# A mixture-of-experts stage on one Trainium2 core: later pairs of experts fetch their tokens by indirect loads and transpositions, from places that a table in DRAM lists

## The chip, the cores and the metric

The kernel runs on one core of one Trainium2 chip. The metric is the device time of one execution in microseconds (us), as the median of several runs. The engines are called PE (TensorE; PEld is its weight load), DVE (VectorE), ACT (ScalarE), POOL (GpSimd) and SP (SyncE, which here only issues the weight loads). Line numbers such as L1071 are those of the kernel before unless the text says that they are of the change.

## What is computed

The program takes 512 tokens of width 1024 in fp32 through two blocks of layers. The first block has a layer of attention with a SwiGLU feed-forward part and a layer of a short convolution with a mixture of experts; the second block has four mixers of other kinds. The change lies in the mixture of experts, cut here to what matters:

```python
D_MODEL, SEQ, N_EXPERTS, TOP_K, D_FF_EXPERT = 1024, 512, 8, 2, 1408

def moe_swiglu(x, w_router, b_router, w_gate, w_up, w_down):
    xt = x.reshape(T, D)
    logits = (xt @ w_router) + b_router
    top_logit, top_e = lax.top_k(logits, TOP_K)
    top_w = jax.nn.softmax(top_logit, axis=-1)
    ...
    def one_block(args):
        e, toks, w = args
        xb = xt[toks]
        h = jax.nn.silu(xb @ w_gate[e]) * (xb @ w_up[e])
        return (h @ w_down[e]) * w[:, None]
    ...
    y = jnp.zeros((T, D)).at[tok_buf].add(out)
```

Each token goes to its two best experts of eight; the two results are weighted and added to the residual stream.

## The kernel before

**Precision.** An fp32 product is made of three matmuls of a faster type: each operand is split into `hi` (rounded, on ACT, L97 and L99) and `lo` (the rest, on DVE, L109 and L113, or on POOL, L111).

**Places.** Each expert has 160 places (`CAP`), of which 128 are the main block and 32 are called the others. If an expert has more tokens than that, `beyond` computes the rest under a branch; here the branch is passed without it. The branch (`most`) is taken by every engine.

**Entry.** `moe` ranks the logits on DVE (L986 to L997: `gt`, `tie`, `rank`, `on`), counts places by matmuls with a triangle (L1002 to L1005, `pos`, `most`), computes the two softmax weights `wts`, and writes four numbers for each token and expert into `know`. Meanwhile the residual stream is transposed to token order (L1022) and split into eight pairs `xth`, `xtl`.

**Dispatch.** `dispatch(e)` serves the experts e and e+1. DVE makes one-hot tiles from `posm` (L1169); 64 matmuls with them (L1178, L1179) pick the tokens out of `xth` and `xtl`; `places` turns each of the 16 results into a hi (ACT), a lo (DVE) and a copy of the others' columns (ACT, L1065). Small matmuls of `know` with the one-hots (L1188, L1191) give the token numbers and weights of each place, and some 16 short DVE operations make `rows` (where results are scattered) and `wt` of them. Pair 0 is dispatched ahead of expert 0; the pairs 2, 4 and 6 within expert 1, 3 and 5, between its up and its down stage.

**Experts.** `up` takes 24 weight loads (16 of 512 KB, 8 of 384 KB), `down` takes 11 of 512 KB. Each load goes from SP's queue into a `raw` tile, is split, and feeds six matmuls for the main block (L1071 to L1073); four matmuls for the others (L1081) use the raw tile itself, and stand collected in groups of four loads. A raw tile is free for the next load when its L1081 matmuls are done. Every third lo of `up` is on POOL (`MO_UP = "pvv"`), every lo of `down` on DVE. Results are scattered by indirect POOL DMAs into `ys` in DRAM (L1232, L1238).

**End.** Ahead of expert 7, POOL loads the sums so far from `ys` (16 loads, L1219) and adds them in pairs (8 additions, L1220); in the middle of the last down stage `mid` transposes them and adds them to the residual stream. Expert 7's own result does not go through `ys`: one-hots `OH` (L1252, L1257) put it in place by matmuls.

The order of the instructions on each engine is set by a tile scheduler, which may move an instruction ahead of others within its window; pools of buffers (`A`: 28 tiles, `T`: 8, PSUM: 8 banks) set the waits.

Of the kernel before, what the change touches and what calls it, by code (L numbers as in the profile page):

```python
# [20 lines left out]
S = 512  # L21
# [914 lines left out]
def moe_begin(s):  # L936
# [15 lines left out]
    m["spot"] = s.ldm("c_spot", (128, 3))  # L952
    m["tok"] = s.ldm("c_tok", (128, NT))
# [17 lines left out]
def moe(s):  # L971
# [25 lines left out]
    nc.vector.tensor_scalar(on, rank, 2.0, None, ALU.is_lt)  # L997
# [18 lines left out]

    xt = []
    for i in range(NT):
        for hf in range(2):
            ps = s.P(("sc", "tp")[hf])  # L1020
            for k in range(4):
                nc.tensor.transpose(ps[:, k * 128:k * 128 + 128], s.xT[4 * hf + k][:, i * 128:i * 128 + 128], s.ident)  # L1022
            h = s.xp.tile([128, 512], F32R, name="xth", tag="xh")
            l = s.xp.tile([128, 512], F32R, name="xtl", tag="xl")
            s.split(ps, h, l, scale=s.rt[:, i:i + 1])
            xt.append((h, l))
# [19 lines left out]
    know = mixp.tile([128, NT, NE, 4], F32R, name="know")  # L1046
    nc.vector.scalar_tensor_tensor(know[:, :, :, 0], sel[1], float(S), m["tok"].unsqueeze(2).to_broadcast(rank3), ALU.mult, ALU.add)
    nc.vector.memset(know[:, :, :, 1].bitcast(F32), 1.0)
    u, v = s.small(rank3, tag="selu"), s.small(rank3, tag="selv")
    nc.vector.tensor_mul(u, sel[0], wts[:, 0].unsqueeze(2).to_broadcast(rank3))  # L1050
    nc.vector.tensor_mul(v, sel[1], wts[:, 1].unsqueeze(2).to_broadcast(rank3))
    nc.vector.tensor_add(u, u, v)
    nc.vector.tensor_copy(know[:, :, :, 2], u)
    nc.vector.tensor_sub(know[:, :, :, 3], u, know[:, :, :, 2].bitcast(F32))

    def places(X, ps, k):
# [7 lines left out]
        s.split(ps[:, 0:128], t[:, 0], t[:, 1], scale=g)  # L1064
        nc.scalar.activation(X[0][:, n * k:n * k + n], ps[:, 128:CAP], AF.Copy, scale=g)  # L1065
# [18 lines left out]
    def up(gu, X, first=()):  # L1084
# [3 lines left out]
        for c, (f0, nb) in enumerate(FBLK):  # L1088
            n = nb * 128
            pp, po, held = [s.P("mm"), s.P("sc")], s.P("o"), []  # L1090
            for k in range(KT):
                i = KT * c + k
                wh, wl, raw = first.pop(0) if first else load3(gu(i)[:, :2 * n], MO_UP[i % len(MO_UP)])
# [27 lines left out]
    def down(dn, H, put, puto, mid=None):  # L1121
# [3 lines left out]
        for f in range(FE):  # L1125
# [9 lines left out]
            if f == FE // 2 and mid is not None:  # L1135
                mid()
# [18 lines left out]

    most = nc.values_load(mosti[0:1, 0:1], min_val=0, max_val=S)
# [4 lines left out]
    def dispatch(e):  # L1161
        YR = float(YROWS)
        tok = s.small((128, 2), tag="etok", bufs=1)

        oh = []
        for i in range(NT):
            t = s.T((128, 2, CAP), F32R)
# [3 lines left out]
        X = [[], []]  # L1171
        for k in range(KT):
            ps = s.P(("st", "o", "tp", "sc", "tp", "sc", "st", "o")[k] if e == 0 else ("st", "o")[k % 2])
            for i in range(NT):
                h, l = xt[2 * i + k // 4]
                q = slice((k % 4) * 128, (k % 4) * 128 + 128)
                r = oh[i].rearrange("p a b -> p (a b)")
                nc.tensor.matmul(ps[:, :2 * CAP], h[:, q], r, start=i == 0, stop=False)  # L1178
                nc.tensor.matmul(ps[:, :2 * CAP], l[:, q], r, start=False, stop=i == NT - 1)  # L1179
            for x in range(2):  # L1180
                places(X[x], ps[:, x * CAP:x * CAP + CAP], k)
        info = []
        for x in range(2):
            ps = s.P("st")
            rows = s.small((128, 3), I32, tag="erow", bufs=4)
            wt = s.small((128, 2), tag="ewt", bufs=4)
            for i in range(NT):
                nc.tensor.matmul(ps[:, 0:4], oh[i][:, x, 0:128], know[:, i, e + x], start=i == 0, stop=i == NT - 1)  # L1188
            for i in range(NT):
                for j in range(4):  # L1190
                    nc.tensor.matmul(ps[32 * j:32 * j + 32, 4:8], oh[i][:, x, 128:].bitcast(F32), know[:, i, e + x].bitcast(F32),  # L1191
                                     start=i == 0, stop=i == NT - 1)
            for b in range(2):
                k4 = s.small((128, 4), tag="ek4")
                t = s.small((128, 1), tag="et")
                nc.vector.tensor_copy(k4, ps[:, 4 * b:4 * b + 4])

                nc.vector.scalar_tensor_tensor(t, k4[:, 1:2], m["spot"][:, b:b + 1], k4[:, 0:1], ALU.mult, ALU.subtract)
                nc.vector.tensor_scalar(t, t, m["spot"][:, b:b + 1], -1.0, ALU.subtract, ALU.mult)
                if b == 0:  # L1200
                    nc.vector.tensor_copy(rows[:, 0:1], t)
                    nc.vector.tensor_scalar(rows[:, 1:2], t, YR, None, ALU.add)
                else:
                    nc.vector.tensor_scalar(rows[:, 2:3], t, 2.0, m["spot"][:, 2:3], ALU.mult, ALU.add)
                nc.vector.tensor_add(wt[:, b:b + 1], k4[:, 2:3], k4[:, 3:4])
                if e + x == NE - 1:

                    f = s.small((128, 1), tag="etf")
                    nc.vector.tensor_scalar(f, t, float(S), -float(S), ALU.is_ge, ALU.mult)
                    nc.vector.tensor_add(tok[:, b:b + 1], t, f)  # L1210
            info.append((rows, wt))
        return X, info, tok


    def load(hf, i):
# [4 lines left out]
        nc.gpsimd.tensor_add(y[0], y[0], y[1])  # L1220
        return y[0]

    for e in range(NE):
        if e == 0:
            X, info, tok = dispatch(0)
        H = up(lambda i, e=e: a["moe_gu"][e * KT * len(FBLK) + i], X[e % 2], ahead)
        rows, wt = info[e % 2]

        def put(x, ps, rows=rows, wt=wt):
            yt = s.T()  # L1230
            nc.scalar.activation(yt, ps, AF.Copy, scale=wt[:, 0:1])
            nc.gpsimd.indirect_dma_start(out=s.ys[:, :], out_offset=bass.IndirectOffsetOnAxis(ap=rows[:, x:x + 1], axis=0),  # L1232
                                         in_=yt[:, :], in_offset=None)

        def puto(ps, rows=rows, wt=wt):
# [5 lines left out]
        if e % 2 and e + 1 < NE:  # L1241
            X, info, tok = dispatch(e + 1)
# [1018 lines left out]
```

## Time and profile before

| | us |
|---|---|
| median of 3 runs | 2858.03 |
| the runs | 2858.03, 2867.24, 2856.01 |
| profiled execution, its own time | 2853.54 |
| its span | 2851.8 |
| experts 0 to 7 in it, from the first L1071 matmul to the last one | 988.5 to 1604.8 |

The profile is of one execution, which is 4.5 us shorter than the median. Its page gives totals over the whole span; the mixture of experts is about a fifth of it and is read from the trace by stretches: an expert begins with its first L1071 matmul. "Idle before" in a row of a group or a timeline is the time in which that engine did nothing ahead of the instruction, and the arrow names what ended it.

### The profile page before, as it was taken

What the parts mean: (1) busy time and instruction counts of PE and PEld (TensorE: products, weight loads), DVE (VectorE), ACT (ScalarE), POOL (GpSimd) and SP (SyncE); (2) the same over time, 40 slices, a digit from 0 to 9 for tenths busy, and PEclk for the clock granted to TensorE, in tenths of its full rate; (3) what the DMA queues carried; (4) which work ended last, traced back from release to release, by engine and by line L of the source; (5) the groups of instructions that cost most, each with busy time, mean ns of one, the idle gap of its engine ahead of it and who ended that gap; (6) DMA issues with size and microseconds to landing.
All of it is one profiled execution on the core that took longest, in us unless ns stands there. A gap on an engine that the chain in (4) does not pass through costs nothing.

```text
span 2851.8 us, 40111 instructions
## 1 busy us (share of the span) xinstructions
PE 2735.7 (96%) x15211; PEld 2168.5 (76%) x15211; DVE 1719.8 (60%) x3194; ACT 1223.3 (43%) x2017; POOL 695.0 (24%) x526
## 2 busy tenths in 40 slices
PE   7989999999999899999998999999999998999999
PEld 6766678888888667676765786778888886788887
DVE  3667669465555465656655747677375456775573
ACT  3555653223322455655654424444243234443342
POOL 3310024222312122323334321032023130122120
PEclk9979999999999899999999999999999998999999
DMA  3210123334432075757757633132333420232322
GB/s 131 93 30 20 37 74 125 102 114 158 174 98 82 24 253 183 279 207 252 254 215 295 188 113 79 32 110 85 107 96 101 131 72 15 83 96 84 108 91 94
DMA packets 119788, 348.36 MB, mean 122 GB/s; under 512 B 16322, under 2 KB 27874, under 8 KB 119076
## 3 DMA queue, kind: packets, MB, share of 16 engines
q1 hardware_dynamic: 106352, 316.66, 33.6%
q0 software_dynamic: 7904, 24.93, 2.5%
q10 hardware_dynamic: 5332, 4.14, 0.5%
q8 instruction: 121, 1.98, 0.3%
q14 instruction: 79, 0.65, 0.1%
HBM read 326.66 MB, written 19.01 MB: 121 GB/s over the span
## 4 chain that ended last, share of the span: by engine, by line
PE 58%; DVE 3%; DMA 2%; ACT 1%; issue 1%; POOL 1%; ACTq 0%; POOLq 0%; SPq 0%; DVEq 0%
PE psmm L138 5%; PE psmm L139 5%; PE psmm L140 5%; PE pso L1081 4%; PE pstp L140 3%; PE pstp L139 3%; PE pstp L138 3%; PE pssc L140 3%; PE pssc L139 3%; PE pssc L138 3%; PE psmm L1071 2%; PE psmm L1072 2%; PE psmm L1073 2%; PE pssc L1073 2%; PE pssc L1072 2%; PE pssc L1071 2%
## 5 line engine op out<-in xcount | busy, mean ns | idle before, releaser
L97 ACT ACTIVATE whi<-raw 128x1024 fp32r<-128x1024 f32 (+5 forms) x663 | 625.7, 947 | 1001.4 <-PE psmm L139 331.6
L113 DVE TENSOR_TENSOR wlo<-raw,whi 128x1024 fp32r<-128x1024 f32 (+4 forms) x581 | 723.3, 1251 | 426.4 <-ACT whi L97 420.0
L111 POOL TENSOR_TENSOR wlo<-raw,whi 128x1024 fp32r<-128x1024 f32 (+3 forms) x82 | 181.4, 2213 | 490.8 <-ACT whi L97 467.7
L138 PE MATMUL psmm<-xh,whi 128*128 128x512 f32 x688 | 273.6, 399 | 10.1 <-ACT xh L99 8.3
L139 PE MATMUL psmm<-xl,whi 128*128 128x512 f32 x688 | 271.8, 395 | 2.3 <-DVE xl L109 2.3
L140 PE MATMUL psmm<-xh,wlo 128*128 128x512 f32 x688 | 271.7, 395 | 1.0 <-DVE wlo L113 1.0
L139 PE MATMUL pssc<-xl,whi 128*128 128x512 f32 x448 | 174.9, 390 | 0.0
L140 PE MATMUL pssc<-xh,wlo 128*128 128x512 f32 x448 | 174.8, 390 | 0.0
L138 PE MATMUL pssc<-xh,whi 128*128 128x512 f32 x448 | 174.6, 390 | 0.0
L138 PEld LDWEIGHTS psmm<-xh,whi 128*128 128x128 f32 x688 | 130.5, 190 | 39.6 <-ACT xh L99 8.3
L1971 POOL TENSOR_TENSOR T<-T 128x512 f32<-128x512 f32 x44 | 57.0, 1296 | 415.8 <-DVE T L1968 352.9
L139 PE MATMUL pstp<-xl,whi 128*128 128x512 f32 x400 | 155.9, 390 | 0.0
L138 PE MATMUL pstp<-xh,whi 128*128 128x512 f32 x400 | 155.7, 389 | 0.0
L140 PE MATMUL pstp<-xh,wlo 128*128 128x512 f32 x400 | 155.7, 389 | 0.0
L139 PEld LDWEIGHTS psmm<-xl,whi 128*128 128x128 f32 x688 | 130.4, 190 | 31.6 <-DVE xl L109 4.9
L1081 PE MATMUL pso<-raw,A 128*32 128x256 f32 x2112 | 153.4, 386 | 0.8 <-ACT A L1065 0.8
L140 PEld LDWEIGHTS psmm<-xh,wlo 128*128 128x128 f32 x688 | 130.4, 189 | 28.9 <-DVE wlo L113 1.5
L111 POOL TENSOR_TENSOR A<-T,A 128x512 fp32r<-128x512 f32 (+1 forms) x78 | 125.6, 1610 | 100.7 <-ACT A L97 100.5
L1071 PE MATMUL psmm<-whi,A 128*128 128x512 f32 (+1 forms) x280 | 114.3, 408 | 9.1 <-ACT whi L97 9.1
L1072 PE MATMUL psmm<-wlo,A 128*128 128x512 f32 (+1 forms) x280 | 113.1, 404 | 10.0 <-DVE wlo L113 8.0
L1081 PEld LDWEIGHTS pso<-raw,A 128*32 128x32 f32 x2112 | 68.1, 110 | 68.4 <-issue 28.5
L254 DVE TENSOR_TENSOR xT<-psmm,xT 128x512 f32<-128x512 f32 x90 | 61.8, 687 | 90.1 <-PE psmm L140 89.6
(651 smaller groups left out, 6151.5 us busy)
## 6 DMA issues: line engine op xcount, KB each, us to landing
raw<-moe_gu SPq DMA_DIRECT2D x128, 512.0 KB
raw<-moe_dn SPq DMA_DIRECT2D x88, 512.0 KB
raw<-w_up_t SPq DMA_DIRECT2D x88, 512.0 KB
raw<-moe_gu SPq DMA_DIRECT2D x64, 384.0 KB
raw<-ffn_gu SPq DMA_DIRECT2D x44, 512.0 KB
raw<-od_w_in_t SPq DMA_DIRECT2D x24, 512.0 KB
raw<-w_in_t SPq DMA_DIRECT2D x24, 512.0 KB
raw<-w_down_t SPq DMA_DIRECT2D x32, 384.0 KB
```

The lines of the kernel that those rows point to most:

```text
L97: nc.scalar.activation(out, x, AF.Copy)
L111: nc.gpsimd.tensor_sub(out, x, h.bitcast(F32))
L113: nc.vector.tensor_sub(out, x, h.bitcast(F32))
L138: nc.tensor.matmul(ps, wh, xh, start=first, stop=False)
L139: nc.tensor.matmul(ps, wh, xl, start=False, stop=False)
L140: nc.tensor.matmul(ps, wl, xh, start=False, stop=last)
L254: s.nc.vector.tensor_add(s.xT[m], ps, s.xT[m])
L1071: nc.tensor.matmul(ps, xh, wh, start=first, stop=False)
L1072: nc.tensor.matmul(ps, xh, wl, start=False, stop=False)
L1073: nc.tensor.matmul(ps, xl, wh, start=False, stop=last)
L1081: last = nc.tensor.matmul(out(j), lhs(k), rhs(raw, j), start=k == 0, stop=k == K - 1)
L1971: nc.gpsimd.tensor_mul(acc[1], acc[1], acc[0])
```

## The change

1. **Ranking first.** The lo's of the token tiles are made to follow `on`. The one-hots are made for pair 0 only, ahead of the branch, in `A` tiles; pair 0 is dispatched as before, without the know matmuls.
2. **A list of places.** A table `tab` in DRAM has a row of four numbers for each place of each expert (place of the result, token, weight). It is filled with empty rows early in the program. After the branch DVE computes each token's place for both of its experts, and POOL scatters eight times 128 rows into the table. POOL also adds `xth` and `xtl` together again (8 additions) and stores them as `xn` in DRAM. Then it loads the table (`kM` the main blocks, `kO` the others), and DVE makes `rows`, `gat`, `wt` and `ltok` for all experts of it.
3. **Later pairs.** At the start of expert 1, 3 and 5 POOL gathers the next pair's tokens from `xn` by five indirect loads. At the fourth load of that expert's down stage `dispatch` transposes them (20 PE transpositions of 128x128), and splits them as before; the others' columns come of one DVE operation for each expert.
4. **Lo's.** Experts 0 and 7 make all lo's of `up` on DVE.
5. **End.** The additions of the early sums go from POOL to DVE, in the last down stage at its third load; `mid`'s transposes come at its seventh load. The `iota512` tile is loaded by POOL ahead of the early loads.

```diff
@@ moe_begin
+    s.tab = s.drp.tile([FAST + 128, 4], F32, name="tab")
+    s.xn = s.drp.tile([2 * S, 512], F32, name="xn")
+    nc.gpsimd.dma_start(s.tab[0:FAST, :], a["c_empty"])
...
@@ moe
-    nc.vector.tensor_scalar(on, rank, 2.0, None, ALU.is_lt)
+    chosen = nc.vector.tensor_scalar(on, rank, 2.0, None, ALU.is_lt)
...
-            s.split(ps, h, l, scale=s.rt[:, i:i + 1])
+            s.hi(h, ps, s.rt[:, i:i + 1])
+            with after(s, chosen):
+                s.lo(l, ps, h, s.rt[:, i:i + 1])
...
+    place = s.small((128, 2, NT), I32, tag="place")
+    for k in range(2):
...
+        for i in range(NT):
+            nc.gpsimd.indirect_dma_start(out=s.tab[:, :], out_offset=bass.IndirectOffsetOnAxis(ap=place[:, k, i:i + 1], axis=0),
+                                         in_=m["info"][:, k, i], in_offset=None)
+
+    for hf in range(2):
+        for i in range(NT):
+            h, l = xt[2 * i + hf]
+            t = s.A((128, 512), F32)
+            nc.gpsimd.tensor_add(t, h.bitcast(F32), l.bitcast(F32))
+            nc.gpsimd.dma_start(s.xn[hf * S + i * 128:hf * S + i * 128 + 128, :], t)
...
+    nc.gpsimd.dma_start(kM, at(0))
+    for j in range(4):
+        nc.gpsimd.dma_start(kO[32 * j:32 * j + 32], at(128))
...
+    def gather(e):
+
+        G = [s.A((128, 512), F32) for _ in range(5)]
+        for n, t in enumerate(G):
+            at = gat[:, e + n // 2, n % 2:n % 2 + 1] if n < 4 else gat[:, e, 2:3]
+            nc.gpsimd.indirect_dma_start(out=t[:, :], out_offset=None, in_=s.xn[:, :], in_offset=bass.IndirectOffsetOnAxis(ap=at, axis=0))
+        return G
+
+    def dispatch(G):
+
+        X, n = [[], []], CAP - 128
+        for hf in range(2):
             for x in range(2):
-                nc.vector.tensor_scalar(t[:, x], m["iota"], posm[:, i, e + x:e + x + 1], None, ALU.is_equal)
-            oh.append(t)
...
+                ps = s.P(("st", "tp")[x])
+                for k in range(4):
+                    nc.tensor.transpose(ps[:, k * 128:k * 128 + 128], G[2 * x + hf][:, k * 128:k * 128 + 128], s.ident)
+                for k in range(4):
+                    places(X[x], ps[:, k * 128:k * 128 + 128], None, 4 * hf + k)
...
     for e in range(NE):
-        if e == 0:
-            X, info, tok = dispatch(0)
-        H = up(lambda i, e=e: a["moe_gu"][e * KT * len(FBLK) + i], X[e % 2], ahead)
-        rows, wt = info[e % 2]
+        if e % 2 and e + 1 < NE:
+            G = gather(e + 1)
+        H = up(lambda i, e=e: a["moe_gu"][e * KT * len(FBLK) + i], X[e % 2], ahead, "v" if e in (0, NE - 1) else MO_UP)
...
-            X, info, tok = dispatch(e + 1)
         if e + 1 < NE:
-            down(lambda f, e=e: a["moe_dn"][e * FE + f], H, put, puto)
+            down(lambda f, e=e: a["moe_dn"][e * FE + f], H, put, puto, (lambda f: f == 3 and Xs.append(dispatch(G))) if e % 2 else None)
...
-    def mid():
-        for k, ps in sums(lambda hf, i: early[hf][i], "st"):
+    def mid(f):
+        if f == 2:
+            for y in chain(*early):
+                nc.vector.tensor_add(y[0], y[0], y[1])
+        if f != 6:
+            return
+        for k, ps in sums(lambda hf, i: early[hf][i][0], "st"):
             s.residual(k, ps)
```

The order of the instructions, at three places. First PE in expert 1, around the dispatch of pair 2. Before, the end of the 64 dispatch matmuls and the know matmuls stand in one block (`psst` and `pso` are PSUM banks, `T` the one-hots):

```order
L1178 MATMUL pso<-T,xth 128x320
L1179 MATMUL pso<-T,xtl 128x320
L1188 MATMUL psst<-know,T 128x4 x4
L1191 MATMUL psst<-know,T 32x4 x16
L1081 MATMUL pso<-raw,A 32x256 x15
```

With the change, transpositions stand singly among the down stage's matmuls, whose lines are now L1067 to L1069, and those of the others, now L1077:

```order
L1068 MATMUL pssc<-wlo,A 128x512
L1235 MATMUL pstp<-pack_all,A 128x128 x4
L1069 MATMUL pssc<-whi,A 128x512
L1067 MATMUL psmm<-whi,A 128x512
L1068 MATMUL psmm<-wlo,A 128x512
L1069 MATMUL psmm<-whi,A 128x512
L1067 MATMUL pssc<-whi,A 128x512
L1068 MATMUL pssc<-wlo,A 128x512
L1235 MATMUL pstp<-pack_all,A 128x128 x4
```

The dispatch block between up and down is gone; the first four transpositions of the pair stand at the second load of expert 1's up stage, and the four of the others (L1240) at the third load of expert 2.

Second, POOL after the branch, with the change (`tab`, `xn`, `kM`, `kO` as above; `place` the table rows, `gat` the gather's):

```order
L1188 DMA tab<-c_c_info,place 1408x4 x4
L1195 TENSOR_TENSOR A<-xth,xtl 128x512 x8
L1188 DMA tab<-c_c_info,place 1408x4
L1196 DMA xn<-A 128x512 x8
L1188 DMA tab<-c_c_info,place 1408x4 x3
L1199 DMA kM<-tab 128x8x4
L1201 DMA kO<-tab 32x8x4 x4
L1225 DMA A<-xn,gat 128x512 x5
L111 TENSOR_TENSOR wlo<-raw,whi 128x1024
```

Before, POOL went from the branch to lo's of expert 0:

```order
L111 TENSOR_TENSOR wlo<-raw,whi 128x1024 x5
L111 TENSOR_TENSOR wlo<-raw,whi 128x768 x2
L111 TENSOR_TENSOR wlo<-raw,whi 128x1024
L1232 DMA ys<-T,erow 2368x512
```

All of the table's traffic is new there, and the lo's of expert 0's up stage are gone from POOL.

Third, DVE in expert 0's up stage with the change, where it first reads the table:

```order
L113 TENSOR_TENSOR wlo<-raw,whi 128x768 x4
L1100 TENSOR_TENSOR T<-pssc,T 128x512
L1104 TENSOR_TENSOR T<-pso,T 128x128
L113 TENSOR_TENSOR wlo<-raw,whi 128x768
L1205 CAST rows<-kM 128x8
L1206 TENSOR_SCALAR rows<-kM 128x8
L1208 CAST gat<-kM 128x8
```

The reads of `kM` stand between lo's of the 384-column loads; nothing of them was there before.

## Rows read from the trace of the kernel before

**Rows 1.** The page, part 1: busy us, share of the span, instructions.

```profile
PE 2735.7 (96%) x15211; PEld 2168.5 (76%) x15211; DVE 1719.8 (60%) x3194; ACT 1223.3 (43%) x2017; POOL 695.0 (24%) x526
```

**Rows 2.** Windows, experts 1, 2, 5 and 6: length, busy (count) by engine, clock, DMA share, GB/s.

```profile
1061.30:1148.00 86.70, 81.86 (x628) 58.88 (x625) 49.27 (x82) 48.62 (x81) 22.55 (x11) 1.00 0.60 210
1148.00:1214.60 66.60, 66.60 (x490) 47.24 (x488) 42.82 (x38) 41.17 (x53) 23.22 (x13) 1.00 0.74 269
...
1369.70:1454.20 84.50, 81.06 (x629) 59.01 (x626) 46.90 (x86) 47.98 (x81) 21.33 (x11) 1.00 0.59 213
1454.20:1522.10 67.90, 67.34 (x490) 47.30 (x488) 44.30 (x39) 41.72 (x53) 24.90 (x13) 1.00 0.75 270
```

**Rows 3.** Windows, up stages of experts 6 and 7.

```profile
1454.20:1500.60 46.40, 45.84 (x331) 32.22 (x329) 30.34 (x26) 28.29 (x37) 22.27 (x11) 1.00 0.73 260
1522.10:1583.30 61.20, 49.28 (x339) 34.84 (x336) 34.30 (x25) 26.50 (x34) 41.10 (x38) 0.89 0.74 275
```

**Rows 4.** Timeline of PE, expert 1: start us, length us, line, operation, idle before.

```profile
1113.21 0.49 PE L1113 MATMUL pstp<-pack_all,T 128*128 128x128 f32 x3
...
1122.46 0.30 PE L1178 MATMUL psst<-T,xth 128*128 128x320 f32 x1
1122.61 0.31 PE L1179 MATMUL psst<-T,xtl 128*128 128x320 f32 x1
...
1133.04 0.61 PE L1188 MATMUL psst<-know,T 128*128 128x4 f32 x4 [0.90 <-ACT A L1065]
...
1136.13 0.61 PE L1188 MATMUL psst<-know,T 128*128 128x4 f32 x4
...
1136.94 2.35 PE L1081 MATMUL pso<-raw,A 128*32 128x256 f32 x34
```

**Rows 5.** Windows, inside expert 5's down stage and expert 7's up stage.

```profile
1420.00:1440.00 20.00, 17.73 (x100) 15.40 (x98) 10.59 (x25) 11.18 (x33) 0.00 (x0) 1.00 0.07 28
1538.60:1560.00 21.40, 11.94 (x99) 7.63 (x97) 11.87 (x8) 6.21 (x9) 16.61 (x22) 0.84 1.01 389
```

**Rows 6.** Groups of PE by shape, expert 1: count, busy us, mean ns, idle before.

```profile
L1113 PE MATMUL pstp<-pack_all,T 128*128 128x128 f32 x11 | 2.4, 277 | 0.0
```

**Rows 7.** Groups of ACT, expert 1.

```profile
L99 ACT ACTIVATE A<-psst,pack_all 128x128 fp32r<-128x128 f32 x8 | 2.9, 363 | 4.6 <-PE psst L1179 4.6
```

**Rows 8.** Groups of POOL, all experts.

```profile
L1232 POOL DMA_INDIRECT ys<-T,erow x14 | 18.2, 1302 | 32.0 <-PE pso L1081 8.5 <-DMA ys<-T,erow 7.0 <-issue 3.9
L1220 POOL TENSOR_TENSOR A<-A 128x512 f32<-128x512 f32 x8 | 12.2, 1540 | 0.0
```

**Rows 9.** Timeline of DVE at the entry.

```profile
963.90 0.74 DVE L109 SCALAR_TENSOR_TENSOR xtl<-pssc,rt,xth 128x512 fp32r<-128x512 f32 x1
...
968.85 0.74 DVE L109 SCALAR_TENSOR_TENSOR xtl<-pssc,rt,xth 128x512 fp32r<-128x512 f32 x1
```

**Rows 10.** Timeline of PE at the first dispatch.

```profile
979.84 0.61 PE L1178 MATMUL psst<-T,xth 128*128 128x320 f32 x1 [6.90 <-DVE T L1169]
```

**Rows 11.** DMA issues: count, KB each, median us to landing.

```profile
vecd<-T POOLq DMA_DIRECT2D x2, 16.0 KB, 1.8
...
ys<-T,erow POOLq DMA_INDIRECT x21, 5.5
```

**Rows 12.** Timeline of DVE, experts 0 and 7.

```profile
1029.78 0.96 DVE L113 TENSOR_TENSOR wlo<-raw,whi 128x768 fp32r<-128x768 f32 x1 [1.28 <-ACT whi L97]
...
1554.39 8.01 DVE L113 TENSOR_TENSOR wlo<-raw,whi 128x768 fp32r<-128x768 f32 x1 [5.05 <-ACT whi L97]
```

**Rows 13.** Timeline of POOL beside the second of these.

```profile
1557.89 3.69 POOL L1220 TENSOR_TENSOR A<-A 128x512 f32<-128x512 f32 x3
```

**Rows 14.** Waits of PE, expert 7's up stage: us in total, times, longest us.

```profile
PE psmm L1072 <- DVE wlo L113: 7.0, 1, 7.0
PE psmm L1071 <- ACT whi L97: 4.9, 1, 4.9
```

**Rows 15.** The page, part 5: groups over the whole span.

```profile
L254 DVE TENSOR_TENSOR xT<-psmm,xT 128x512 f32<-128x512 f32 x90 | 61.8, 687 | 90.1 <-PE psmm L140 89.6
```

More of the change, by code (lines that the diff above doesn't have):

```diff
@@ L1082, in others, with up @@
         held.clear()
-    def up(gu, X, first=()):
+    def up(gu, X, first=(), les=MO_UP):
         H, HO = [], s.A((128, FE * 32), F32)
@@ L1092, in up @@
                 i = KT * c + k
-                wh, wl, raw = first.pop(0) if first else load3(gu(i)[:, :2 * n], MO_UP[i % len(MO_UP)])
+                wh, wl, raw = first.pop(0) if first else load3(gu(i)[:, :2 * n], les[i % len(les)])
                 for x in range(2):
@@ L1134, in down @@
                        lambda j: po[32 * j:32 * j + 32, 0:256])
-            if f == FE // 2 and mid is not None:
-                mid()
+            if mid is not None:
+                mid(f)
         for x in range(2):
@@ L1154, in moe @@
     (s.rawp, s.spp), more, s.more = rest, s.more, None
+    oh = []
+    for i in range(NT):
+        t = s.A((128, 2, CAP))
+        for x in range(2):
+            nc.vector.tensor_scalar(t[:, x], m["iota"], posm[:, i, x:x + 1], None, ALU.is_equal)
+        oh.append(t.rearrange("p a b -> p (a b)"))
     most = nc.values_load(mosti[0:1, 0:1], min_val=0, max_val=S)
@@ L1159, in moe @@
     s.more = more
[L1161 to L1165, printed above, removed]
+    X = [[], []]
+    for k in range(KT):
+        ps = s.P(("st", "o", "tp", "sc", "tp", "sc", "st", "o")[k])
         for i in range(NT):
-            t = s.T((128, 2, CAP), F32R)
-            for x in range(2):
-                nc.vector.tensor_scalar(t[:, x], m["iota"], posm[:, i, e + x:e + x + 1], None, ALU.is_equal)
-            oh.append(t)
[L1171 to L1182, printed above, removed]
-        for x in range(2):
[L1184 to L1212, printed above, removed]
@@ new lines, in moe @@
+            h, l = xt[2 * i + k // 4]
+            q = slice((k % 4) * 128, (k % 4) * 128 + 128)
+            nc.tensor.matmul(ps[:, :2 * CAP], h[:, q], oh[i], start=i == 0, stop=False)
+            nc.tensor.matmul(ps[:, :2 * CAP], l[:, q], oh[i], start=False, stop=i == NT - 1)
+        for x in range(2):
+            places(X[x], ps[:, x * CAP:x * CAP + 128], ps[:, x * CAP + 128:x * CAP + CAP], k)
+    big = s.small(rank3, tag="big")
+    nc.vector.tensor_scalar(big, pos, float(CAP), float(2 * FAST), ALU.is_ge, ALU.mult)
@@ new lines, in moe @@
+    nc.vector.tensor_add(big, big, pos)
+    nc.vector.tensor_add(big, big, m["base"][:, 0].unsqueeze(1).to_broadcast(rank3))
+    nc.vector.tensor_copy(m["info"][:, :, :, 2], wts)
+    place = s.small((128, 2, NT), I32, tag="place")
+    for k in range(2):
+        u = s.small(rank3, tag="selu")
+        nc.vector.tensor_mul(u, sel[k], big)
+        d = s.small((128, NT), tag="dest")
+        nc.vector.tensor_reduce(d, u, AX.X, ALU.add)
+        nc.vector.tensor_scalar(place[:, k], d, m["spot"][:, 3:4], None, ALU.min)
+        for i in range(NT):
+            nc.gpsimd.indirect_dma_start(out=s.tab[:, :], out_offset=bass.IndirectOffsetOnAxis(ap=place[:, k, i:i + 1], axis=0),
+                                         in_=m["info"][:, k, i], in_offset=None)
```

96 lines of the change are left out of this document (58 added, 38 removed).

## The prediction

> **What bounds the kernel now.** The page's first part comes first [rows 1]: TensorE (PE) is busy for 96% of the span, POOL for 24%. Time can only be won by taking work or waits off PE, and another engine's work costs something only where PE ends up behind it. But that is a mean over the kernel's stages, and the change lies in one of them, so I cut the trace at the first weight matmul (L1071) of each expert [rows 2].
>
> In that table the experts are not alike. The even ones after expert 0 (2, 4 and 6) take 67.8 us in the mean of three (the first 66.6, the last 67.9); in these two PE is busy for 99 to 100% of the time and the DMA share is 0.74 and 0.75: the bound is PE. The odd ones that dispatch the next pair (1, 3 and 5) take 85.8 in the mean of three (the first 86.7, the last 84.5), with as many weights and matmuls of their own, and the DMA share falls to 0.59 to 0.60. Expert 7 dispatches nothing, but its up stage takes 61.2 us, where that of expert 6 takes 46.4, which is also the mean of experts 1 to 6 [rows 3].
>
> Where the odd experts' 18.0 us go is seen in expert 1's timeline [rows 4]: 64 dispatch matmuls (8 k-tiles, 4 token tiles, hi and lo), one every 0.147 us (1122.46 to 1122.61), make 9.4 us; two runs of know matmuls, 0.8 us each (1136.13 to 1136.94), 1.6; waits like that of 0.90 us for ACT to empty a bank at 1133.04. The remainder comes behind it: raw tiles are freed by the L1081 matmuls, which stand behind the dispatch in PE's order, so the next weights are asked for late. In the middle of expert 5's down stage the queues move 28 GB/s [rows 5], against 210 to 270 over whole experts.
>
> **The change, part by part.**
>
> *Pairs 2, 4, 6.* If all that belongs to the dispatch disappeared, an odd expert would be as long as an even one: 3 × 18.0 = 54.0 us. In its place PE gets 20 transpositions of 128x128 per pair. L1113 is the same operation: three in a row take 0.49 us, one alone 0.28 in the mean [rows 4, 6], so one every 0.11 us: 20 × 0.11 = 2.2. Waits on them I set at 1.0 per pair, one of the present waits for ACT. So 3 × (18.0 − 3.2) = **−44.4**. Bounds: no waits, −47.4; all of ACT's new work on the path, 16 hi of 0.363 us [rows 7] = 5.8 per pair, −30. I stay near the first end, since ACT is busy for only 41.7 of the 67.9 us of expert 6 [rows 2], and the new order spreads the transpositions over several loads. The first four already stand at the head of the odd expert, which costs nothing if the gather has landed (the last rival).
>
> The five indirect loads of a pair take POOL about 1.3 us each by the scatter's row [rows 8], 6.5 us, ahead of the expert's first lo on POOL. POOL is idle for three quarters of the time, so I cost them at nothing; without that cover it would be 3 × 6.5.
>
> *Entry and expert 0.* Today `on` ends behind seven xtl lo's, one every 0.66 us (963.90 to 968.85 is the first to the last, with ranking steps between) [rows 9]. PE needs `on` for L1002, the branch needs `mosti` after it. In the new order no lo is ahead of `on`, but four lo's come before `mosti`, partly in the time that DVE now waits for PE. I take −3.3, bounds 0 and −4.6 (7 × 0.66). The one-hots now come before the branch; PE waited 6.90 us for the first of them [rows 10], most of it the branch itself, and its banks are still emptied by a DVE that must pass the branch, so I count no more. Expert 0's own know matmuls go: 2 × 0.8 = −1.6.
>
> Against this, POOL gets eight scatters into the table, eight additions of 128x512, eight stores and five loads. DVE reads the table in up(0), behind the lo of the fifth 384-column load, and all that follows on DVE waits with it. The scatters go one after another, each waiting until the last has landed. For 16-byte rows the trace has no price; nearest are a small POOL store, 1.8 us to landing, and the scatter of 2 KB rows, 1.3 us on POOL and 5.5 to landing [rows 8, 11]. With 1.0 to 1.3 us of issue that is 2.8 to 6.8 per scatter; eight of them, 12 us of additions and 4 us of stores put the table's load some 38 to 70 us behind the branch. DVE gets there some 45 us behind it (today's DVE row of that place is at 1029.78 [rows 12], the branch ends just before 979.84, and the entry is shorter), with about 4 us of finished lo's ahead of PE. Nearest is the small store: +2, bounds 0 and +21.
>
> The eight additions cost more. At 1554.39 a DVE lo of 128x768, which takes 0.96 us undisturbed, lasted 8.01 us [rows 12], while POOL ran additions and one lo back to back (the last three additions in 3.69 us) [rows 13]. Expert 0 now has all its lo's on DVE, and POOL's eight additions stand in one row, 12.2 us by today's mean of 1.54 [rows 8]. I take half, since PE has L1077 matmuls of earlier loads to go on with: +6, bounds 0 and +12.
>
> The Trainium skill ("SBUF — State Buffer", section "Who interferes with whom") says that a DVE instruction with two SBUF inputs and a GpSimd instruction that reads SBUF exclude each other for the length of an instruction. By that alone the DVE lo would wait for one addition, the term would be about +1.5 and the whole forecast 4.5 us lower; the row of 8.01 us shows more than one instruction's wait, so the row decides.
>
> Sum of this part: −3.3 − 1.6 + 2 + 6 = **+3.1**.
>
> *Expert 7.* Its up stage stands 14.8 us over the others' 46.4. PE's waits there are 7.0 us for one DVE lo (the one just told of) and 4.9 for ACT's hi [rows 14]. POOL's additions move to DVE in the down stage, and this expert's lo's all to DVE, so the first goes. But 16 loads of `ys` (256 KB each) still run beside the weights, and for 21.4 us the DMA share is 1.01 [rows 5]; `iota512` joins them. So I let 3 us of the 14.8 stand: −11.8. Eight additions on DVE are 8 × 0.687 (an addition of this shape, L254) [rows 15] = 5.5 us, half of it in DVE's waits: +2.5. Together **−9.3**, bounds 0 and −14.8.
>
> *The rest.* Some places in the first layer's attention have PE's rows in another order, with the same instructions; and the empty table is filled behind that layer. Both 0.
>
> **Sum.** −44.4 + 3.1 − 9.3 = −50.6. The profiled execution takes 2853.5 us (span 2851.8), so 2802.9; the median of the three runs is 4.5 above it, so **2807**.
>
> **The rivals.**
>
> *ACT and DVE bound the new dispatch.* Its 16 hi and 16 lo share the down stage with the weight halves, and PE waits for banks as it does at 1133.04. All of 5.8 us per pair: 3 × 5.8 = 17, 2824. Against it: ACT's room.
>
> *Expert 7 stays starved.* If the queues and not POOL set its 61.2 us, it keeps them: +11.8, 2819. For it: the share of 1.01. Against it: the longest wait is DVE's.
>
> *The table comes late.* At 6.8 us per scatter: 21 in place of 2, 2826. It would show as a DVE wait at the first read of kM.
>
> *The odd experts are bound by loads.* If weights, not dispatch, set 85.8, nothing is won there: 3.1 − 9.3 gives about 2852, no change. Against it: even experts move the same bytes in 67.8 us, at a share of 0.74.
>
> *Slower: the gathers land late.* PE goes in order, so transpositions at the head of an odd expert hold back every matmul behind them, and POOL's first lo stands behind the gather as well. The gather waits for A tiles that PE must free. To be slower than before it has to cost over 17 us a pair; at 24 it is 3 × 24 = 72 more, 2879. Against it: in POOL's order the later gathers stand ahead of the previous expert's scatters, and the first is due at the end of up(0), some 20 us before it is needed.
>
> **How the numbers follow.** Forecast 0.60; dispatch bound 0.12; expert 7 starved 0.12; table late 0.08; bound by loads 0.05; gathers late 0.03. About 0.5% (14.3 us) can be told from no change with this kernel. The first four are faster: 0.92; the fifth is the same: 0.05; the last is slower: 0.03. The forecast's own bounds, taken in part, reach from 2782 to about 2818; with the next three, and two of them in part at once, the range is **2782 to 2832**, and the last two cases are left out.
>
> **What would show it.** Right: odd experts of about 71 us at a DMA share of 0.7, few PE waits at the transpositions (L1235, L1240); an up stage of expert 7 under 50 us; a DVE wait of some us at the first read of kM, and long DVE lo's beside POOL's L1195 in expert 0. Wrong: odd experts over 76 us, with PE waiting for ACT or DVE in their down stage; PE's waits at L1235 ended by a DMA; an expert 0 of over 85 us; or a stretch outside the experts that is 5 us longer.

## The result and the profile after

The changed kernel takes 2826.97 us in the median of four runs (2823.22 to 2834.34), the kernel before 2858.02: a ratio of 0.9886, 95% interval 0.9854 to 0.9917. It is faster by 31 us, where 51 were forecast. A second measurement beside other kernels gave 2828.48 us in the median of six, ratio 0.9883 (0.9864 to 0.9901). The profiled execution is the slowest of the first four, 2834.34 us, so its span tells less than its stretches: the two profiled spans differ by 19 us (2851.8 and 2832.6), the medians by 31.

The page, part 1, answers to [rows 1]: PE's share of the span is what it was.

```profile
PE 2722.8 (96%) x14791; PEld 2149.2 (76%) x14791; DVE 1708.1 (60%) x3125; ACT 1209.3 (43%) x1969; POOL 696.3 (25%) x549
```

Cut in the same way as [rows 2], by the first weight matmul of an expert (now L1067), the stretches of experts 0, 1, 2, 4, 5 and 6 (length, busy and count by engine, clock, DMA share, GB/s):

```profile
996.30:1075.00 78.70, 71.99 (x497) 49.81 (x495) 51.48 (x61) 42.70 (x60) 33.90 (x33) 0.96 0.69 245
1075.00:1144.10 69.10, 69.10 (x508) 49.16 (x505) 45.74 (x49) 44.45 (x63) 21.63 (x12) 1.00 0.71 261
1144.10:1214.80 70.70, 69.38 (x496) 47.50 (x492) 43.41 (x42) 41.71 (x56) 27.77 (x17) 1.00 0.74 275
...
1284.20:1357.80 73.60, 70.25 (x496) 48.74 (x492) 42.41 (x43) 42.19 (x57) 27.91 (x16) 0.98 0.73 264
1357.80:1427.20 69.40, 69.40 (x508) 49.28 (x504) 42.97 (x49) 43.18 (x64) 22.34 (x11) 1.00 0.73 261
1427.20:1496.00 68.80, 67.85 (x496) 47.92 (x492) 43.83 (x44) 41.40 (x55) 20.66 (x11) 1.00 0.75 266
```

and that of expert 7's up stage, against [rows 3]:

```profile
1496.00:1558.80 62.80, 51.83 (x351) 34.76 (x348) 36.09 (x43) 26.62 (x35) 15.13 (x24) 0.89 0.78 281
```

| stretch, us | before | after | moved | forecast |
|---|---|---|---|---|
| start to expert 0's first matmul | 988.5 | 996.3 | +7.8 | -3.3 |
| expert 0 | 72.9 | 78.8 | +5.9 | +6.4 |
| experts 1, 3, 5 | 257.4 | 207.8 | -49.6 | -44.4 |
| experts 2, 4, 6 | 203.3 | 213.2 | +9.9 | 0 |
| expert 7 (first to last matmul) | 82.7 | 86.1 | +3.4 | -9.3 |
| the rest | 1246.9 | 1250.4 | +3.5 | 0 |

The experts' stretch, 616.3 us, is now 585.9: 30.4 us less. The odd experts are as short as hoped; the even ones, which the change was thought not to touch, are longer; expert 7 has gained nothing. The last column takes the prediction's terms apart by stretch.

**Odd experts.** The new dispatch hardly shows. In PE's timeline (start, length, line, operation, idle before) the three groups in expert 1's down stage and the last, for the others, in expert 2 run without a wait, as did the first at 1076.98:

```profile
1131.35 0.60 PE L1235 MATMUL pstp<-pack_all,A 128*128 128x128 f32 x4
...
1133.18 0.60 PE L1235 MATMUL pstp<-pack_all,A 128*128 128x128 f32 x4
...
1137.14 0.66 PE L1235 MATMUL psst<-pack_all,A 128*128 128x128 f32 x4
...
1148.81 0.60 PE L1240 MATMUL psst<-pack_all,A 128*128 128x128 f32 x4
```

**Even experts.** The last row above is where their loss begins. L1240 makes the others' tile of the next pair, X[0], and it stands in the third load of expert 2. Expert 2's first L1077 matmuls need that tile. They run at 1153.51, 9.4 us into the expert, and until then none of its own raw tiles comes free. In the kernel before, the first of them (L1081) came 4.7 us into expert 2. The first row is of the kernel before, the others are of the changed one:

```profile
1152.76 1.48 PE L1081 MATMUL pso<-raw,A 128*32 128x256 f32 x18
...
1153.51 1.93 PE L1077 MATMUL pso<-raw,A 128*32 128x256 f32 x32
...
1157.92 1.93 PE L1077 MATMUL pso<-raw,A 128*32 128x256 f32 x32
```

By the trace SP issues no weights from 1144.4 to 1154.2 (before, the longest pause at that place was 6.4 us, 1147.1 to 1153.5). The queues are nearly empty in the five microseconds after 1150, and again at the same place in expert 4. The first row is the same place in expert 2 of the kernel before:

```profile
1153.00:1158.00 5.00, 5.00 (x43) 2.98 (x36) 5.00 (x3) 2.03 (x3) 4.05 (x2) 1.00 0.65 200
...
1150.00:1155.00 5.00, 5.00 (x44) 3.51 (x46) 4.51 (x5) 1.34 (x2) 3.80 (x3) 1.00 0.15 56
1290.00:1295.00 5.00, 5.00 (x45) 3.53 (x47) 3.57 (x7) 2.49 (x3) 1.44 (x1) 1.00 0.17 66
```

Part of the price is seen as waits of PE a few loads later. In expert 4 (total, times, longest us):

```profile
PE psmm L1068 <- POOL wlo L111: 2.3, 1, 2.3
PE psmm L1068 <- DVE wlo L113: 0.5, 1, 0.5
```

Over experts 2, 4 and 6 PE's idle time rose from 2.6 to 5.6 us, which is 3.0 of the +9.9. The rest is time that the profile books as busy PE, and no run splits it further.

**Expert 0.** The long lo of [rows 12, 13] is there again, and longer. POOL's eight additions, and the DVE lo that began two microseconds after them:

```profile
986.70 1.09 POOL L1188 DMA_INDIRECT tab<-c_c_info,place  x1 [31.98 <-DVE place L1186]
992.42 0.99 POOL L1188 DMA_INDIRECT tab<-c_c_info,place  x1 [4.64 <-DMA tab<-c_c_info,place]
994.82 0.97 POOL L1188 DMA_INDIRECT tab<-c_c_info,place  x1 [1.41 <-DMA tab<-c_c_info,place]
...
998.66 9.88 POOL L1195 TENSOR_TENSOR A<-xth,xtl 128x512 f32<-128x512 f32 x8
...
1031.00 0.95 POOL L1199 DMA_DIRECT2D kM<-tab  x1 [1.42 <-DMA tab<-c_c_info,place]
```

```profile
1000.82 8.82 DVE L113 TENSOR_TENSOR wlo<-raw,whi 128x1024 fp32r<-128x1024 f32 x1 [0.78 <-ACT whi L97]
```

PE waits 5.82 us for that lo. Its matmuls of 512 columns then come every 0.43 us (0.23 where the granted clock is 1.00), and the granted clock is at the lower of its two levels (0.50, that is 1.2 of 2.4 GHz; third column from the right in the last row, a window):

```profile
1009.69 0.80 PE L1068 MATMUL psmm<-wlo,A 128*128 128x512 f32 x1 [5.82 <-DVE wlo L113]
...
1011.13 0.63 PE L1069 MATMUL pssc<-whi,A 128*128 128x512 f32 x1
1011.56 0.63 PE L1067 MATMUL psmm<-whi,A 128*128 128x512 f32 x1
...
1009.70:1014.10 4.40, 4.40 (x10) 3.46 (x11) 3.41 (x3) 1.06 (x1) 4.39 (x8) 0.50 0.80 207
```

The table is not late: its load is issued at 1031.00 (last POOL row), 45 us behind PE's first matmul after the branch (985.78), and DVE reads it at 1042.01 with no wait.

**Expert 7.** DVE stands still for 12.71 us, in front of the first of the additions that came over from POOL:

```profile
1527.18 0.69 DVE L1300 TENSOR_TENSOR A<-A 128x512 f32<-128x512 f32 x1 [12.71 <-DMA A<-ys]
```

They were written at the third load of the last down stage, but the scheduler has put all eight among the lo's of up(7), and six of them ahead of the lo of its first 384-column load. They need what POOL loads from `ys`, and that is late, since three scatters go one after another and the loads go behind them. The third row names ACT, but by the trace the second scatter landed only at 1510.97 and the third at 1519.19, 2.8 us before the first load:

```profile
1496.05 1.26 POOL L1264 DMA_INDIRECT ys<-T,rows  x1 [29.82 <-ACT T L1263]
1503.49 0.97 POOL L1264 DMA_INDIRECT ys<-T,rows  x1 [6.18 <-DMA ys<-T,rows]
1511.71 1.66 POOL L1270 DMA_INDIRECT ys<-T,rows  x1 [7.25 <-ACT whi L97]
1522.02 4.86 POOL L1252 DMA_DIRECT2D A<-ys  x9 [8.64 <-issue]
```

PE waits 10.97 us, and while and after it waits, the clock is at the lower level (windows of 5 us, clock in the third column from the right):

```profile
1520.00:1525.00 5.00, 0.00 (x0) 0.00 (x0) 0.00 (x0) 0.31 (x1) 2.98 (x6) 0.81 0.99 359
1525.00:1530.00 5.00, 0.00 (x0) 0.00 (x0) 1.80 (x3) 0.00 (x0) 3.49 (x8) 0.50 0.95 330
1530.00:1535.00 5.00, 4.23 (x16) 2.46 (x16) 5.00 (x6) 1.01 (x2) 2.67 (x5) 0.50 1.03 392
1535.00:1540.00 5.00, 5.00 (x25) 2.73 (x22) 3.00 (x5) 0.00 (x0) 1.57 (x3) 0.82 0.33 130
```

### The profile page after: what moved, and what is told of

Its sections match the earlier page's. It is cut to its first block, busy times and chain, and to the rows that moved or that the text cites. A ratio compares the mean times of both kernels' runs of the same rounds, so it can differ in the third digit from the quotient of the medians.

```text
span 2832.6 us, 39198 instructions
## 1 busy us (share of the span) xinstructions
PE 2722.8 (96%) x14791; PEld 2149.2 (76%) x14791; DVE 1708.1 (60%) x3125; ACT 1209.3 (43%) x1969; POOL 696.3 (25%) x549
## 4 chain that ended last, share of the span: by engine, by line
PE 57%; DMA 3%; DVE 2%; ACT 1%; issue 1%; POOL 1%; SPq 0%; ACTq 0%; POOLq 0%; DVEq 0%
PE psmm L138 5%; PE psmm L139 5%; PE psmm L140 5%; PE pso L1077 4%; PE pstp L140 3%; PE pstp L139 3%; PE pstp L138 3%; PE pssc L140 3%; PE pssc L139 3%; PE pssc L138 3%; PE psmm L1068 2%; PE psmm L1067 2%; PE psmm L1069 2%; PE pssc L1068 2%; PE pssc L1069 2%; PE pssc L1067 2%
## 5 line engine op out<-in xcount | busy, mean ns | idle before, releaser
L113 DVE TENSOR_TENSOR wlo<-raw,whi 128x1024 fp32r<-128x1024 f32 (+3 forms) x596 | 717.7, 1210 | 410.7 <-ACT whi L97 392.9
L111 POOL TENSOR_TENSOR wlo<-raw,whi 128x1024 fp32r<-128x1024 f32 (+3 forms) x67 | 142.1, 2121 | 337.6 <-ACT whi L97 296.2
L1077 PE MATMUL pso<-raw,A 128*32 128x256 f32 x2112 | 151.5, 384 | 0.0
L1077 PEld LDWEIGHTS pso<-raw,A 128*32 128x32 f32 x2112 | 65.3, 109 | 69.2 <-issue 32.2
L1067 PE MATMUL psmm<-whi,A 128*128 128x512 f32 (+1 forms) x280 | 114.0, 407 | 1.0 <-ACT whi L97 1.0
```

What stands on the lines that cost most here:

```text
L111: nc.gpsimd.tensor_sub(out, x, h.bitcast(F32))
L113: nc.vector.tensor_sub(out, x, h.bitcast(F32))
L1067: nc.tensor.matmul(ps, xh, wh, start=first, stop=False)
L1077: last = nc.tensor.matmul(out(j), lhs(k), rhs(raw, j), start=k == 0, stop=k == K - 1)
```

## The experiments

The stretches carry the verdicts here, since executions of one kernel differ by up to 18 us (2854.48 to 2872.57 in seven runs of the kernel before). In the profiles of one kernel the experts' stretch differs by less: 2.2 us in two profiles of the changed kernel, 4.7 in three of the kernel before.

**1. The additions of expert 7 held back.**

```diff
-            nc.vector.tensor_sub(out, x, h.bitcast(F32))
+            s.last_lo = nc.vector.tensor_sub(out, x, h.bitcast(F32))
...
         if f == 2:
-            for y in chain(*early):
-                nc.vector.tensor_add(y[0], y[0], y[1])
+            with after(s, s.last_lo):
+                for y in chain(*early):
+                    nc.vector.tensor_add(y[0], y[0], y[1])
```

> Only edit against the changed kernel: DVE's eight additions of the early sums may not be issued before the lo of the third load of the last down stage. Theory A (in the changed kernel they were moved ahead of up(7)'s lo's, and DVE stands 12.7 us behind ys loads that have not landed): PE's wait of 11.0 us in expert 7's up stage goes, with the half-clock stretch behind it; up(7) falls from 62.8 to 48 to 51 us, the kernel to about 2813 to 2816. Rival B (the ys loads starve the weights): up(7) stays at 58 us or more, PE then waits for ACT's hi behind DMA, and the kernel gains under 4 us on 2827.

Expert 7's up stage fell from 62.8 to 47.6 us and PE has no wait in it, with the same 16 loads beside the weights at a DMA share of 0.90:

```profile
1497.40:1545.00 47.60, 47.60 (x335) 31.49 (x332) 28.50 (x30) 26.68 (x36) 12.92 (x21) 1.00 0.90 332
```

The whole expert takes 70.7 us (86.1), the experts together 568.4 (585.9). So theory A holds and the loads do not starve this stage. The kernel's time does not show it clearly: 2824.86 us, ratio 0.9873 (0.9834 to 0.9911), outside the 2813 to 2816 expected, and only 2 us under the 2827, as the rival had it; in this profile the time before expert 0 was 999.7 and after expert 7 1253.8, both over 3 us longer than in the changed kernel's. It is the stretch and PE's missing wait that decide.

**2. The additions back on POOL.**

```diff
-                nc.vector.tensor_add(y[0], y[0], y[1])
+                nc.gpsimd.tensor_add(y[0], y[0], y[1])
```

> Only edit against the changed kernel: the eight additions of the early sums go back to POOL (with all lo's of expert 7 still on DVE). Theory A (DVE stands behind the loads): DVE's 12.7 us wait goes; but POOL's additions now lock DVE's lo's for up to about 10 us, so up(7) is 54 to 60 us, the kernel 2818 to 2825. Rival B (loads starve the weights): up(7) stays at 60 us or more. If POOL's additions do not hold DVE up, up(7) is 48 to 51.

Up(7) took 60.9 us, by the rival's mark; but the wait has another place. Waits of PE there:

```profile
PE psst L1144 <- POOL A L1300: 9.0, 2, 8.3
```

The transpositions of `mid` had come forward into up(7) too, and now PE itself stands before them. For up(7) the run does not tell theory A from starved loads, which the first one does. But it shows a long lo once more. While POOL's eight additions ran, a DVE lo of 128x768 took 4.32 us, and the DVE addition just ahead of it, one of whose inputs lies in PSUM (`psst`), took no longer than elsewhere (0.687 in [rows 15]):

```profile
1528.91 9.89 POOL L1300 TENSOR_TENSOR A<-A 128x512 f32<-128x512 f32 x8
...
1534.69 0.69 DVE L254 TENSOR_TENSOR xT<-psst,xT 128x512 f32<-128x512 f32 x1 [10.67 <-PE psst L1144]
1535.30 4.32 DVE L113 TENSOR_TENSOR wlo<-raw,whi 128x768 fp32r<-128x768 f32 x1
```

The time was 2827.7 us, ratio 0.9879 (0.9838 to 0.992).

**3. xn from ACT.**

```diff
             with after(s, chosen):
                 s.lo(l, ps, h, s.rt[:, i:i + 1])
+            t = s.A((128, 512), F32)
+            nc.scalar.activation(t, ps, AF.Copy, scale=s.rt[:, i:i + 1])
+            nc.gpsimd.dma_start(s.xn[hf * S + i * 128:hf * S + i * 128 + 128, :], t)
...
-            nc.gpsimd.tensor_add(t, h.bitcast(F32), l.bitcast(F32))
-            nc.gpsimd.dma_start(s.xn[hf * S + i * 128:hf * S + i * 128 + 128, :], t)
```

> Only edit against the changed kernel: xn is made by ACT from PSUM at the entry (eight copies with a scale) and stored there, in place of POOL's eight additions of hi and lo after the branch. Theory A (POOL's run of additions locks DVE's lo for 8.8 us and PE waits 5.8 us): that wait goes with the half-clock stretch behind it, expert 0 falls from 78.8 to 70 to 73 us, the entry grows by 0 to 3 us; the kernel about 2820 to 2823. Rival B (expert 0 is long because its loads are asked for late and the table's traffic competes): expert 0 stays at 76 us or more.

Expert 0 took 76.8 us, which looks like the rival. But the long lo is gone, and DVE waits at another place: the scheduler put the first read of the table ahead by some loads, and there it comes too early.

```profile
1014.06 1.23 DVE L113 TENSOR_TENSOR wlo<-raw,whi 128x1024 fp32r<-128x1024 f32 x1 [0.35 <-ACT whi L97]
...
1024.21 0.22 DVE L1202 CAST rows<-kM 128x8 int32<-128x8 f32 x1 [7.55 <-DMA kM<-tab]
```

This is the prediction's rival of the late table, met in another kernel: 7.55 us. Time 2829.47 us, ratio 0.988 (0.9843 to 0.9917).

**4. All lo's of the up stages on DVE.**

```diff
-MO_UP = "pvv"
+MO_UP = "v"
```

> Only edit against the changed kernel: all lo's of every up stage on DVE, so that POOL has only DMA issues in the experts. Theory A (experts 2, 4 and 6 grew from 66.5, 68.9 and 67.9 to 70.8, 73.6 and 68.8 us because a POOL lo stands behind a scatter that waits until the one before has landed): those three fall to 66 to 68.5 us, 8 to 12 us in the sum, the kernel to about 2816 to 2819. Rival B (they grew because weights come late): their sum stays within 3 us of 213. Rival C (DVE becomes the bound in the experts): odd and even experts grow by 2 us or more each.

Experts 2, 4 and 6 took 72.8, 74.0 and 73.3 us, 220.0 together: more, not less. Theory A of this run falls. A POOL lo behind a scatter is what PE was seen to wait for, but without POOL's lo's the loss grew. The odd experts stayed (207.1), so DVE is not the bound there. What this run has in common with the changed kernel is L1240 in the third load and the first L1077 matmuls behind it, here 10.9 us into expert 2. Time 2834.21 us, ratio 0.9905 (0.9868 to 0.9942).

**5. The changed kernel again.**

> The changed kernel itself, beside the three others on the same chip. Stretches as in its first profile: experts 2, 4 and 6 together 213 us, expert 0 78 to 79, expert 7 85 to 86, odd experts 208; the time before expert 0 and after expert 7 shows how far these two vary from one execution to the next (996.3 and 1250.4 us in the first profile, 988.5 and 1246.9 in that of the kernel before).

Expert 0 78.5, odd 207.8, even 213.0, expert 7 84.4; the time before expert 0 was 1000.0, after expert 7 1249.0. The stretches of the experts repeat within 2 us.

**6. The others first in the dispatch.**

```diff
-        if k == 0:
+        if k == 0 and not X:
...
         X, n = [[], []], CAP - 128
+        ps = s.P("st")
+        for k in range(4):
+            nc.tensor.transpose(ps[:, k * 128:k * 128 + 128], G[4][:, k * 128:k * 128 + 128], s.ident)
+        for x in range(2):
+            X[x].append(s.A((128, KT * n), F32))
...
         for hf in range(2):
...
-        ps = s.P("st")
-        for k in range(4):
-            nc.tensor.transpose(ps[:, k * 128:k * 128 + 128], G[4][:, k * 128:k * 128 + 128], s.ident)
...
```

> Only edit against the changed kernel: in the dispatch of the later pairs the four transpositions of the others and DVE's two products come first, ahead of the main blocks, instead of last. Theory D (the even experts grew because their first L1077 matmuls wait for the others' tile X[0], which is made only in their third load, at 1148.8; so raw tiles are held and SP issues no weights from 1144.4 to 1154.2): that hole shrinks to 6.5 us or less, experts 2, 4 and 6 fall from 213 to 203 to 207 us in the sum, the kernel gains 6 to 10 us on the changed kernel. Rival (the weights come late for want of DMA bandwidth, or POOL's lo stands behind scatters): the sum stays at 211 us or more.

Theory D holds. The first L1077 matmuls of expert 2, which starts at 1141.8 here, come 4.8 us into it instead of 9.4, the pause in SP's issues at that place is 5.5 us instead of 9.8, and PE is busy through the whole expert:

```profile
1146.64 1.05 PE L1077 MATMUL pso<-raw,A 128*32 128x256 f32 x10
```

```profile
1147.00:1152.00 5.00, 5.00 (x44) 2.97 (x36) 3.72 (x5) 2.93 (x5) 3.38 (x2) 1.00 0.72 237
...
1141.80:1210.30 68.50, 68.50 (x490) 47.67 (x488) 41.80 (x43) 41.23 (x58) 28.12 (x17) 1.00 0.78 282
```

Experts 2, 4 and 6 took 68.5 us each, 205.6 together. Time 2818.89 us, ratio 0.9858 (0.9841 to 0.9875), 9.6 us under the changed kernel beside it. Not all of that is the even experts: expert 7 also came out shorter, 78.7 us. The additions of the early sums are not pinned here, but more lo's stand ahead of the first of them, and DVE's wait for `ys` is 3.67 us in place of 12.71 (PE's 4.3 in place of 10.97):

```profile
1517.16 0.69 DVE L1301 TENSOR_TENSOR A<-A 128x512 f32<-128x512 f32 x1 [3.67 <-DMA A<-ys]
```

**7. xn from ACT, and the table read late.** The third run, with all of DVE's reads of the table in a function `table`, called after up(0):

```diff
+        s.load_lo = s.last_lo
...
+        if e == 0:
+            with after(s, s.load_lo):
+                table()
```

> Against the changed kernel: xn from ACT as in the third run, and DVE's reads of the table held back until behind the lo of the last load of up(0). Theory A (POOL's additions cost expert 0 some 8 us, and the third run only turned this wait into one of DVE for kM, 7.55 us): both waits go, expert 0 takes 69 to 72 us; the kernel gains 6 to 9 us on the changed kernel. Rival (expert 0 is bound by its late loads): 76 us or more.

Expert 0 took 69.4 us (78.5 beside it). Neither the long lo nor the wait for kM is left: five lo's of its up stage take 5.77 us where POOL's additions ran before, and the reads follow one another.

```profile
1008.33 5.77 DVE L113 TENSOR_TENSOR wlo<-raw,whi 128x1024 fp32r<-128x1024 f32 x5 [3.91 <-ACT whi L97]
...
1036.75 1.91 DVE L113 TENSOR_TENSOR wlo<-raw,whi 128x768 fp32r<-128x768 f32 x2 [0.32 <-ACT whi L97]
1038.58 0.17 DVE L1204 CAST rows<-kM 128x8 int32<-128x8 f32 x1
```

The entry did not get longer by ACT's copies that one could tell: the first matmul of expert 0 is at 997.9, against 1000.0 and 996.3 in the two profiles of the changed kernel. Time 2821.79 us, ratio 0.9865 (0.9845 to 0.9885), 6.7 us under the changed kernel beside it.

**8. All three together** (the edits of runs 1, 6 and 7).

> The additions of the early sums pinned in the last down stage, the others first in the dispatch, xn from ACT and late reads of the table, all together. If the three losses are separate, the stretch from the first to the last matmul of the experts falls from 586 us to the sum of what each gave: about 586 - 15 - 8 - 7 = 556 us, 60 us under the kernel before (616.3), and the kernel to about 2798 to 2804. If they share a cause (weights that come late move the wait elsewhere), it stays above 563.

The experts' stretch fell to 559.4 us, 57 under the kernel before, and the kernel to 2805.19 us (2801.41 to 2814.33): ratio 0.9811, 95% interval 0.9793 to 0.9829. It beats both kernels, the one before by 56 us and the changed one by 23. The stretch is 3.4 us over the 556 expected, and the time 1 us over its 2798 to 2804. What the three gave alone (15.4 us in expert 7, 7.4 in the even experts, 9.1 in expert 0) would have made about 554 of the 585.9, so the three losses are separate but for some 5 us. Of these, expert 0 (72.2) kept a wait of 2.3 us for ACT.

```profile
989.40:1061.60 72.20, 69.91 (x491) 48.01 (x489) 45.28 (x65) 43.43 (x66) 18.76 (x18) 0.98 0.69 243
1131.40:1200.20 68.80, 68.80 (x491) 47.69 (x489) 42.09 (x43) 41.31 (x58) 28.28 (x17) 1.00 0.77 281
...
1476.10:1548.80 72.70, 71.35 (x494) 47.56 (x492) 49.25 (x57) 36.71 (x47) 16.88 (x27) 1.00 0.80 286
```

**9 and 10. The kernel before, profiled twice more.**

> The kernel before, profiled a second time. If the change's other order of PE's rows in the first layer costs time, the stretch before expert 0 is again within 2 us of 988.5; if the 991 to 1000 us of the changed kernel and its variants are only other executions (the clock granted in the attention heads), it falls somewhere in 988 to 1000. The experts themselves should repeat: 616 us, odd 257, even 203, within 2.

> The kernel before, profiled a third time, for the same question as the ninth run: within 2 us of 988.5 before expert 0 if the order of the first layer costs time, anywhere in 988 to 1000 if not; the experts 616 us within 2.

Before expert 0: 988.7 and 993.6 us; experts 619.4 and 621.0 (odd 258.5 and 262.5, even 203.2 and 202.7); the rest 1251.1 and 1243.4. So the experts are a little longer than in the first profile, which makes the odd experts' gain 51 to 55 us, and the rest spreads over 8 us without any change. The stretch before expert 0 spreads too: three profiles of the kernel before lie at 988.5 to 993.6, the nine of the changed kernel and its variants at 989.4 to 1000.0. The 993.6 lies outside the 2 us that the mark for a cost of the order allowed. Still, whether the other order in the first layer costs some microseconds stays open; what can be seen is that the granted clock between 100 and 200 us was 0.80 in the changed kernel's first profile and 0.76 in its second (1000.0), 0.85 in two of the kernel before and in run 8 (whose stretch is 989.4), and 0.81 in the third of the kernel before (993.6).

## Why the prediction was right, and where its sum was not

The direction and the range (2782 to 2832) held. The point was 20 us too low (2807 against 2826.97). The sum is near on the odd experts and, by terms that offset one another, on expert 0; elsewhere it is wrong.

*Pairs 2, 4, 6: right.* -44.4 forecast, -49.6 measured, beyond the end of -47.4 called the bound with no waits at all; two further profiles of the kernel before put its odd experts at 258.5 and 262.5, so that stretch alone varies by 5 us. Part of the surplus is that four of a pair's 20 transpositions stand in the next even expert (3 × 4 × 0.11 = 1.3). The price of a transposition was right: four start to end in 0.60 us, and no waits on them. The rivals of a dispatch bound by ACT and DVE, of experts bound by loads, and of late gathers did not come.

*What this part left out: the even experts.* The step that failed is the one that set the odd experts' target at the even experts' length and left the even ones at zero. L1240 at the third load of the next expert was read and written down, but no price was put on what waits for it. The even experts grew by 9.9, and run 6 gives 7.4 back (213.0 to 205.6) by order alone; the 2.3 that are left over 203.3 were not looked into.

*Entry and expert 0.* The additions were named with the right mechanism and undersized: +6 forecast (bounds 0 and +12), and run 7, without them and with the table read late, gives 9.1 back (78.5 to 69.4). 5.8 of it is the wait for one lo; matmuls at the lower clock behind it, some 2 us, were not in the sum. The table cost 0, not +2. Its scatters were about as slow as forecast (2.4 to 6.1 us from one to the next where nothing else stood between, against 2.8 to 6.8), but DVE came 56 us behind the branch instead of 45; run 3, where it came earlier, paid 7.55. That expert 0 still comes out near its forecast (+5.9 against +6.4) is luck: eight more of its dispatch matmuls now stand ahead of its first weight matmul (56 of 64, before 48), which moves 8 × 0.147 = 1.2 us into the entry, and PE's waits for ACT fell from 2.3 to 0.4. The entry gained less than -3.3: from the ranking's first comparison to expert 0's first matmul it was 25.3 us before (963.22 to 988.5) and is 24.9 (971.40 to 996.3). Of that, the way to the first dispatch matmul is shorter by 2.2, and the dispatch behind it longer by 1.8: the eight matmuls more, and 17 instead of 12 that come every 0.27 us at a granted clock of 0.50, and not every 0.147 at 1.00.

The Trainium skill ("SBUF — State Buffer", section "Who interferes with whom") says that a DVE instruction with two SBUF inputs and a GpSimd instruction that reads SBUF contend for a pair of ports, which is an exclusive lock. The prediction took the length of one instruction from it, and the trace does not agree with that as a bound on the wait: the lo was held for 8.82 us, until eight additions of 1.24 us each (9.88 / 8) were through. Why it was held for the whole row no run tried. The trace agrees on who is held: run 2's DVE addition with one input in PSUM was not. Runs 3 and 7 show that without POOL's additions no lo in expert 0's stretch is held like that (the longest takes 1.23 us in run 3 and 1.62 in run 7, beside a lo on POOL).

*Expert 7: wrong, -9.3 against +3.4.* The step that failed is that the eight additions on DVE cost 5.5 us in the down stage, half of it in DVE's waits. Their length was right (0.69 us), their place was not: they were taken to stand where the code has them, and the scheduler had put all eight into up(7). Run 1 puts them back, and up(7) takes 47.6 us against the 49.4 that the sum had. The rival that came nearest in time, the queues starving up(7), named the wrong cause: in run 1 the same loads run beside the weights and PE never waits.

*The rest.* Forecast 0 and measured +3.5 after the experts; the start to expert 0's first matmul is +7.8 against -3.3. That lies ahead of the ranking's first comparison (963.22 before, 971.40 now), and its cause stays open (runs 9 and 10).

*Signs.* Of the signs of being right, the odd experts came (69.0 to 69.4 us at a DMA share of 0.71 to 0.73, no wait of PE at L1235 or L1240), and the long lo beside L1195. An up stage of expert 7 under 50 us and a DVE wait at the first read of kM did not come. Of the signs of being wrong one came: a stretch outside the experts that is 5 us longer.

*Chances.* The forecast's 0.60 with its own range to 2818 did not come. The time lies just above where the rivals of one more loss each lay (2819 to 2826), but it came there by none of their mechanisms: one of the two larger losses was no rival, and the other had another cause than its rival named. That the range held is therefore in part luck.

## What to carry to other kernels

When work is moved to an engine that goes in order, price its place in that engine's final order and the last data it waits for, and not its length alone: here DVE stood 12.7 us in front of the first of eight additions of 0.69 us, which cost PE 11 us, and holding the eight back gave 15 us in that stage. When a producer is broken into pieces, look for the small piece that frees a buffer: the others' tile was the least of the dispatch's work, and because it came last it held the raw tiles of a whole group of loads. An edit that removes one wait should be read again in the new trace before it is judged: runs 2 and 3 gave 1.5 and 2.0 us in their expert (86.1 to 84.6, 78.8 to 76.8), since another wait stood in the place of the one removed.

## What was not expected of the hardware

PE's two long waits cost more than themselves: during the waits of 5.82 and 10.97 us, from about 1004 and 1520 on, the granted clock fell to 0.50, and behind them PE worked at that level for some five microseconds, in which matmuls of 512 columns came every 0.43 us instead of 0.23.

Small scatters were at their best cheaper than their nearest rows. The page gives eight of 128 rows of 16 bytes a median of 2.1 us to landing, against 5.5 for rows of 2 KB [rows 11], but the trace holds the landing of only three (2.1, 2.1 and 5.4). Small loads of the same table took 5.6:

```profile
tab<-c_c_info,place POOLq DMA_INDIRECT x8, 2.1
...
kO<-tab POOLq DMA_DIRECT2D x4, 4.0 KB, 5.6
```
